# Moving modulation blocks, regrouping the solved values of a recurrent scan, and re-pacing projections in a two-layer hybrid block

## The chip, the cores and the metric

The kernel runs on one core of a Trainium2 chip. The metric is the device time of one execution in microseconds (us), and the median of several runs is compared. Engines are named as in the profile: PE is TensorE's matmul side and PEld its weight loads, DVE is VectorE, ACT is ScalarE, POOL is GpSimd, SP is SyncE, whose queue issues most transfers. PEclk is the granted share of TensorE's clock: 1.0 is 2.4 GHz and 0.5 is 1.2 GHz, the only two levels, so a value between them is a mean over a stretch.

## The reference

Two layers work on 512 tokens (256 of context, 256 latent) of width 1024. In each layer:

- `m = silu(cond) @ ada_w + ada_b` gives six modulation vectors per conditioning (shift, scale and gate of the mixer, shift, scale and gate of the MLP), 6 x 1024 columns, so 12 blocks of 512 columns.
- `h = rms_norm(x) * (1 + scale) + shift`, then `p = h @ w_in`, some 13,000 columns.
- Three mixers read `p`: an SSD (Mamba) mixer, an RWKV-7 scan in both directions over 16 heads of 64, and a gated delta net (GDN) in both directions over 8 heads of 128.
- `mixed = g_m*(y_m@w_bm) + g_r*(y_r@w_br) + g_g*(y_g@w_bg)` with sigmoid gates out of `p`; `x += gate1 * (mixed @ w_out)`; then `x += gate2 * (relu(h2@w_ff1)^2 @ w_ff2)` with `h2` modulated again.

Layer 1 needs only the 256 latent tokens from the mixers' outputs on, so there most products behind the scans are half as long. All is float32; large products are made of three passes with operands split in a high and a low part.

## The kernel before

**Order.** Every part is a Python generator that yields after a piece of work. `weave` (line 30) merges generators: it always steps the one with the smallest `(steps done + 0.5) / weight`, and the tile framework schedules the merged program on the engines. Each engine then runs its instructions in a fixed order.

**Stages of a layer**, as `run` (line 1580) writes them:

1. The pre-stage (drain at line 1644): `scalars` (decays), `first` (the low-rank parts of RWKV, its gates and the first 36 steps of the RWKV chain `rc`) and `ada(li, range(4, 12), ...)`, the modulation blocks 4 to 11 of this layer. Blocks 0 to 3 (shift and scale of the mixer) are made earlier: layer 0's before the layers, layer 1's in the MLP of layer 0.
2. The mix (line 1648): `rc` with weight 400 (about 460 steps are left in layer 0), `gc`, the GDN chain, with weight 195 (some 224 steps), and `ahead`, 44 projections with weight 48.
3. `merge` of the RWKV and the GDN branch, woven with `mamba_chain`; then `merge` of the Mamba branch; then `w_out`.
4. `mlp`: four groups of eight `w_ff1` and eight `w_ff2` products.

**`ada`** (line 235). One block loads four 512 KB pieces of `ada_w` (`araw`), multiplies them as 32 float32 products with 32 weight columns, copies the sums (`adaS`), transposes them and adds the bias into `modT`. In the pre-stage its loads are issued by POOL, with two buffers; elsewhere by SP with four.

**`proj` and `ahead`**. `proj` loads 1024 x 128 of `w_in` in two pieces (`wraw`), splits each (ACT writes `whi`, POOL writes `wlo`) and makes 24 products over 512 or 256 tokens. `ahead` (line 1249) makes 24 gate projections ("t", with a tanh), 8 of Mamba's z ("z") and 12 with a convolution ("c"), and stores them in device memory for the stage behind the mix. They come in eight groups of three t, one z, and one or two c.

**`rwkv_scan`** (line 837). One of 16 units (head pair x half) is eight steps, each with two directions `d` and two heads `e`: four products `rA<-U,W` give the solved values; each of the four results stands in its own 32 partitions of `rA`, and four ACT copies (lines 852 and 853) bring them into `U`; four products `rA<-U,KT` give the next state; DVE multiplies by the decay into the next step's `U`. The profile counts each of these float32 products as two instructions.

Of the kernel before, what the change touches and what calls it, by code (L numbers as in the profile page):

```python
# [8 lines left out]
F32 = mybir.dt.float32  # L9
F32R = mybir.dt.float32r  # L10
AF = mybir.ActivationFunctionType
ALU = mybir.AluOpType
# [17 lines left out]
def weave(*parts):  # L30

    live = [[g, n, 0] for g, n in parts]
    while live:
        p = min(live, key=lambda e: (e[2] + 0.5) / e[1])
        p[2] += 1
        try:
            next(p[0])
        except StopIteration:
            live.remove(p)
            continue  # L40
        yield


def drain(g):
    for _ in g:
        pass

L0, N0, N1, W_S, W_R, W_F, W_G = 3, 16, 20, 24, 400, 48, 195
W_A = 4


class Hybrid:
# [182 lines left out]
    def ada(self, li, blocks, pool, bufs=4, tag=None):  # L235

        condT = self.condT
        if condT is None:
            condT = pool.tile([128, 8, 32], F32, name="condR")
            self.dma(condT, self.condD)  # L240
        for b in blocks:
            new = (lambda nm: self.gen([128, 128], nm)) if tag is None else (lambda nm: self.sp.tile([128, 4, 128], F32, tag=tag, name=nm)[:, 0])
            ps = new("adaps")
            for kk in range(4):
                raw = pool.tile([128, 2, 512], F32, tag="araw", name="araw", bufs=bufs)
                (self.nc.gpsimd if tag else self.nc.sync).dma_start(out=raw, in_=self.ins["ada_w"][li][256 * kk : 256 * kk + 256, 512 * b : 512 * b + 512].rearrange("(k p) n -> p k n", p=128))
                for k in range(2):
                    for j in range(4):
                        self.mm(ps[32 * j : 32 * j + 32, :], condT[:, 2 * kk + k, :], raw[:, k, 128 * j : 128 * j + 128],
                                start=(kk + k == 0), stop=(kk == 3 and k == 1))  # L250
            S = pool.tile([128, 128], F32, tag="adaS", name="adaS", bufs=bufs // 2)
            self.nc.scalar.copy(S, ps)
            pt = new("adaT")
            self.tr(pt, S)
            v = pt.rearrange("p (j r) -> p j r", r=32)[:, :, 0:2]
            o = 48 * li + 4 * b
            self.tt(self.modT[:, li, 4 * b : 4 * b + 4, :], v, self.bcol[:, o : o + 4].unsqueeze(2).to_broadcast([128, 4, 2]), ALU.add)
            yield
# [578 lines left out]
    def rwkv_scan(self, li, hp, q, S, Unext):  # L837

        nc, rp = self.nc, self.rp
        skip = q == 0 and li == NL - 1  # L840
        U, W, KT, PC = S["U"], S["W"], S["KT"], S["PC"]
        sl = slice(256 * q, 256 * q + 256)
        A = self.rA
        y = None
        for s in range(8):
            cc = (s, 7 - s)
            for d in range(2):
                for e in range(2):
                    o = slice(64 * d + 32 * e, 64 * d + 32 * e + 32)
                    self.mm(A[o, 0:64], W[:, e, 0, d, cc[d]], U[:, e, cc[d]])  # L850
            for d in range(2):
                nc.scalar.copy(U[96:128, 0, cc[d]], A[64 * d : 64 * d + 32, 0:64])  # L852
                nc.scalar.copy(U[32:64, 1, cc[d]], A[64 * d + 32 : 64 * d + 64, 0:64])  # L853

            Un, cn = (U, (s + 1, 6 - s)) if s < 7 else (Unext, (0, 7))
            f = 0 if cn[0] < cn[1] else 1
            if not (q == 1 and s == 7):
                for d in range(2):
                    y0 = 64 if d == f else 128
                    for e in range(2):  # L860
                        self.mm(A[64 * e : 64 * e + 64, y0 : y0 + 64], KT[:, e, 8 * d + cc[d]], U[:, e, cc[d]])


            if not skip and s % 4 == 3:
                for e in range(2):
                    for d in range(2):
                        g = (s // 4) ^ d
                        y0 = 192 + 128 * g + 64 * e
                        for i in range(4):
                            self.mm(A[32 * i : 32 * i + 32, y0 : y0 + 64], W[:, e, 1, d, 4 * g + i], U[:, e, 4 * g + i])  # L870
                if y is None:
                    y = rp.tile([128, 4, 64], F32, tag="ry", name="ry")
                    yf = y.rearrange("p a b -> p (a b)")
                    nc.scalar.copy(yf, A[:, 192:448])
                else:
                    self.tt(yf, yf, A[:, 192:448], ALU.add)

            if not (q == 1 and s == 7):
                lo, hi = min(cn), max(cn)
                i, j = 8 * f + cc[f], 8 * (f + 1) + cc[1 - f]  # L880
                for e in range(2):
                    o = slice(64 * e, 64 * e + 64)
                    dec = fap(PC[o], [[j - i, 2], [0, 64]], i)
                    self.vlast = self.tt(Un[o, e, lo : hi + 1 : hi - lo], A[o, 64:192].rearrange("p (d v) -> p d v", d=2), dec).ins
            yield
        if skip:
            return
        gT = rp.tile([128, 256], F32, tag="gT", name="gT")
        self.load(gT, self.gD[li][128 * hp : 128 * hp + 128, sl])
        st = rp.tile([128, 3, 4], F32, tag="rst", name="rst")  # L890
        nc.vector.tensor_reduce(out=st[:, 0], in_=y, axis=AX.X, op=ALU.add)
        self.ts(st[:, 0], st[:, 0], 1.0 / 64)
        self.tt(y, y, st[:, 0].unsqueeze(2).to_broadcast([128, 4, 64]), ALU.subtract)
        ys = rp.tile([128, 4, 64], F32, tag="ryT", name="rys")
        self.act(ys, y, AF.Square)
        nc.vector.tensor_reduce(out=st[:, 1], in_=ys, axis=AX.X, op=ALU.add)
        self.ts(st[:, 1], st[:, 1], 1.0 / 64, ALU.mult, 64e-5, ALU.add)
        self.rsqrt(st[:, 2], st[:, 1], 4)
        self.tt(y, y, st[:, 2].unsqueeze(2).to_broadcast([128, 4, 64]))
        yield  # L900
        py = self.gen([128, 256], "ryT")
        for j in range(2):
            self.tr(py[:, 128 * j : 128 * j + 128], yf[:, 128 * j : 128 * j + 128])
        yT = rp.tile([128, 256], F32, tag="ryT", name="ryT")
        self.act(yT, py, AF.Identity, bias=self.pc["r_ln_b"][:, hp : hp + 1], scale=self.pc["r_ln_g"][:, hp : hp + 1])
        self.tt(yT, yT, S["bT"], ALU.add, eng=nc.gpsimd)
        self.tt(yT, yT, gT, eng=nc.gpsimd)
        self.dma(self.yD[li][1][128 * hp : 128 * hp + 128, sl], yT)
        yield
# [334 lines left out]
        self.dma(self.yD[li][2][128 * h : 128 * h + 128, t0:], yT[:, t0:])  # L1244
        yield

    N_AH = 44

    def ahead(self, li):


        nc, gp = self.nc, self.gp
        t0 = 256 if li == NL - 1 else 0
        todo = []
        for i in range(8):
            todo += [("t", 3 * i + j) for j in range(3)] + [("z", i)] + [("c", 3 * i // 2 + j) for j in range(1 + i % 2)]
        for kind, n in todo:
            new = lambda: gp.tile([128, T], F32, tag="gzs", name="ahead")
            rows = slice(128 * n, 128 * n + 128)
            if kind == "z":  # L1260
                o = new()
# [318 lines left out]
    def run(self):  # L1580
# [4 lines left out]
        with ExitStack() as ctx:  # L1585
# [38 lines left out]
            for li in range(dbg.get("layers", NL)):  # L1624
                end = ExitStack()
                with lay[li] as s:
                    with ExitStack() as s2:
# [8 lines left out]
                        with self.pool(f"pre{li}") as pre:  # L1636
# [4 lines left out]
                                yield from weave((lo, 10 - L0), (itake(rc, N0), N0))  # L1641
                                yield from weave((self.rwkv_gates(li, pre), 8), (itake(rc, N1), N1))

                            drain(weave((self.scalars(li, pre), W_S), (first(), 18 + N0 + N1), (self.ada(li, range(4, 12), pre, 2, "gsc"), W_A)))
                        self.ig = s2.enter_context(self.pool(f"ig{li}"))
                        self.gp = s2.enter_context(self.pool(f"gp{li}"))
                        gc = self.gdn_chain(li) if "g" in which else iter(())
                        drain(weave((rc, W_R), (self.ahead(li), W_F), (gc, W_G)))
                    mixed_p = s.enter_context(self.pool(f"mx{li}"))
                    mixed = mixed_p.tile([128, 8, T], F32, name="mixed")  # L1650
                    flip = [0]
# [27 lines left out]
                    mf = end.enter_context(self.psum(f"mf{li}", 4, side="right"))  # L1679
                    x = xp.tile([128, 8, T], F32, name="x")  # L1680
                    self.dma(x, xD)
                    drain(self.merge(li, 0, "w_bm", bp, mixed, False, eng))
                    self.raw_bufs, self.wp, self.mp = 3, wf, mf
                    with self.pool(f"wo{li}") as op:
                        drain(self.w_out(li, x, mixed, op, eng))
                    self.dump(f"x1_{li}", x)
                if li < NL - 1:
                    wp = open_layer(li + 1)
                with end:
                    with self.pool(f"fm{li}") as mp:  # L1690
                        with self.pool(f"ae{li}") as ap:
                            ad = self.ada(1, range(4), ap) if li == 0 else iter(())
                            if li < NL - 1:
                                self.params(li + 1, ap)
                            drain(weave((self.mlp(li, x, mp, eng), self.N_F), (ad, 4)))
                        self.dump(f"x2_{li}", x)
                        if li < NL - 1:
                            self.dma(xD, x)
# [5 lines left out]
def itake(g, n):  # L1704

    for _ in range(n):
        try:
            next(g)
        except StopIteration:
            return  # L1710
        yield
# [27 lines left out]
```

## Time and profile before

| | |
|---|---|
| Median of 3 runs | 4058.03 us (4052.08 to 4059.62) |
| Profiled execution | 4078.95 us, its span 4077.2 us, mean granted clock 0.865 |
| Busy share of the span | PE 85%, PEld 64%, DVE 59%, POOL 54%, ACT 43% |
| Transfers | 468.79 MB, mean 115 GB/s |

The span is what the profiler saw between the first and the last instruction; 1.75 us lie around it. A busy share counts an instruction from its start to its modelled end, and matmuls overlap, so PE's share says how seldom it stood still, not how near it was to its peak. The stages can be told apart by their instructions: in layer 0 the pre-stage runs to about 300 us, the mix to 1515, the merges and `w_out` to 1857, the MLP to 2270; in layer 1 the pre-stage ends at about 2490 and the mix at 3610.

### The profile page before, as it was taken

What the parts mean: (1) busy time and instruction counts of PE and PEld (TensorE: products, weight loads), DVE (VectorE), ACT (ScalarE), POOL (GpSimd) and SP (SyncE); (2) the same over time, 40 slices, a digit from 0 to 9 for tenths busy, and PEclk for the clock granted to TensorE, in tenths of its full rate; (3) what the DMA queues carried; (4) which work ended last, traced back from release to release, by engine and by line L of the source; (5) the groups of instructions that cost most, each with busy time, mean ns of one, the idle gap of its engine ahead of it and who ended that gap; (6) DMA issues with size and microseconds to landing.
All of it is one profiled execution on the core that took longest, in us unless ns stands there. A gap on an engine that the chain in (4) does not pass through costs nothing. (4 is left out here: it accounts for less than half of the span.)

```text
span 4077.2 us, 71668 instructions
## 1 busy us (share of the span) xinstructions
PE 3455.8 (85%) x25827; PEld 2598.3 (64%) x25827; DVE 2421.4 (59%) x5836; ACT 1758.9 (43%) x4025; POOL 2191.6 (54%) x2882
## 2 busy tenths in 40 slices
PE   5778989999989869988999677788878878768798
PEld 3556666666766645666887446666667666546697
DVE  2557766776667746644333635776666766746465
ACT  2345545555556422223222334545555545322343
POOL 3448765856758403433443445767656857324354
PEclk7879989989989758989999876878988888669799
DMA  6753434434433126444332573334334433154464
GB/s 199 208 155 88 105 92 103 102 97 104 108 98 96 48 53 175 129 142 145 96 103 73 153 227 94 95 89 112 94 95 104 100 94 85 39 140 129 131 170 131
DMA packets 789775, 468.79 MB, mean 115 GB/s; under 512 B 243116, under 2 KB 736172, under 8 KB 788908
## 3 DMA queue, kind: packets, MB, share of 16 engines
q1 hardware_dynamic: 780204, 430.66, 39.6%
q0 software_dynamic: 9216, 33.56, 2.7%
q8 instruction: 203, 3.33, 0.4%
q14 instruction: 152, 1.25, 0.1%
HBM read 384.64 MB, written 79.43 MB: 114 GB/s over the span
## 5 line engine op out<-in xcount | busy, mean ns | idle before, releaser
L75 POOL TENSOR_TENSOR wlo<-wraw,whi 128x512 fp32r<-128x512 f32 (+1 forms) x576 | 948.5, 1649 | 840.0 <-ACT whi L198 793.4
L198 ACT CAST whi<-wraw 128x512 fp32r<-128x512 f32 (+1 forms) x608 | 454.8, 751 | 920.6 <-PE pj L87 282.8
L87 PE MATMUL pj<-hhi,whi 128*128 128x512 f32 (+2 forms) x1664 | 676.1, 406 | 78.9 <-ACT ahead L72 21.6
L87 PE MATMUL pj<-hhi,wlo 128*128 128x512 f32 (+2 forms) x1664 | 659.0, 396 | 7.8 <-POOL wlo L75 7.8
L87 PE MATMUL pj<-hlo,whi 128*128 128x512 f32 (+2 forms) x1664 | 649.5, 390 | 2.8 <-DVE hlo L84 2.8
L87 PEld LDWEIGHTS pj<-hhi,whi 128*128 128x128 f32 (+1 forms) x1664 | 348.4, 209 | 160.4 <-ACT ahead L72 25.0
L87 PEld LDWEIGHTS pj<-hhi,wlo 128*128 128x128 f32 (+1 forms) x1664 | 346.7, 208 | 78.7 <-POOL wlo L75 10.6
L75 POOL TENSOR_TENSOR cpr<-cpr 128x512 f32<-128x512 f32 (+1 forms) x288 | 365.1, 1268 | 50.1 <-ACT cpr L72 39.6
L87 PEld LDWEIGHTS pj<-hlo,whi 128*128 128x128 f32 (+1 forms) x1664 | 349.1, 210 | 55.5 <-DVE hlo L84 4.5
L72 ACT ACTIVATE cpr<-cin,ptab 128x512 f32<-128x512 f32 (+1 forms) x360 | 240.1, 695 | 38.9 <-POOL cpr L75 30.4
L75 DVE TENSOR_TENSOR invP<-invP,invT 128x60 f32<-128x60 f32 (+24 forms) x992 | 213.9, 216 | 24.6
L75 DVE TENSOR_TENSOR invT<-invP,invL 128x60 f32<-128x60 f32 (+24 forms) x992 | 205.8, 207 | 26.1 <-DMA invL<-invM 1.5
L87 PE MATMUL rA<-U,W 128*32 128x64 f32 x3584 | 142.9, 255 | 89.7 <-DVE U L75 84.0
L75 DVE TENSOR_TENSOR U<-rA,PC 64x128 f32<-64x128 f32 x480 | 137.2, 286 | 129.8 <-PE rA L87 89.6
L75 DVE TENSOR_TENSOR fr<-fr 128x512 f32<-128x512 f32 (+1 forms) x64 | 135.4, 2124 | 85.1 <-ACT fr L72 85.1
L87 PEld LDWEIGHTS rA<-U,W 128*32 128x32 f32 x3584 | 79.1, 122 | 164.6 <-DVE U L75 104.3
L75 POOL TENSOR_TENSOR invT<-invY,invL 128x60 f32<-128x60 f32 (+24 forms) x496 | 164.8, 332 | 32.5 <-DMA invL<-invM 7.4
L75 POOL TENSOR_TENSOR invY<-invY,invT 128x60 f32<-128x60 f32 (+24 forms) x496 | 167.4, 338 | 25.8
L87 PE MATMUL f<-fhi,whi 128*128 128x512 f32 (+1 forms) x512 | 171.8, 340 | 6.2 <-ACT whi L198 4.2
L87 PE MATMUL rA<-U,KT 128*64 128x64 f32 x1920 | 130.0, 261 | 54.6 <-ACT U L853 53.3
L852 ACT COPY U<-rA 32x64 f32<-32x64 f32 x512 | 102.9, 201 | 169.7 <-PE rA L87 150.6
L87 PE MATMUL f<-hhi,whi 128*128 128x512 f32 (+1 forms) x512 | 173.5, 343 | 2.7 <-ACT whi L198 1.6
(398 smaller groups left out, 7973.9 us busy)
## 6 DMA issues: line engine op xcount, KB each, us to landing
wraw<-in_w_in SPq DMA_DIRECT2D x412, 256.0 KB
wraw<-in_w_ff SPq DMA_DIRECT2D x128, 512.0 KB
araw<-in_ada_w POOLq DMA_DIRECT2D x64, 512.0 KB, 5.6
invL<-invM SPq DMA_DIRECT2D x192, 128.0 KB
araw<-in_ada_w SPq DMA_DIRECT2D x32, 512.0 KB
lD<-lo SPq DMA_DIRECT2D x64, 256.0 KB
dupD<-ahead SPq DMA_DIRECT2D x40, 256.0 KB
rcs<-lD SPq DMA_DIRECT2D x32, 256.0 KB
```

The lines of the kernel that those rows point to most:

```text
L72: return self.nc.scalar.activation(out, in_, func, bias=bias, scale=scale, **kw)
L75: return (eng or self.nc.vector).tensor_tensor(out=out, in0=a, in1=b, op=op)
L87: return self.nc.tensor.matmul(out, lhsT, rhs, start=start, stop=stop, **kw)
L198: self.nc.scalar.copy(hi, raw)
L852: nc.scalar.copy(U[96:128, 0, cc[d]], A[64 * d : 64 * d + 32, 0:64])
```

## The change

There are three parts.

- **Modulation blocks.** `ada` leaves the pre-stage of both layers. Layer 0's blocks 4 to 7 are woven into the merge of the Mamba branch and 8 to 11 into `w_out`; layer 1's blocks 4 to 11 go into the MLP of layer 0, beside its blocks 0 to 3. All loads of these blocks are now issued by SP.
- **Solved values.** The results of both directions of one head stand side by side in the 32 partitions where `U` wants them, so two ACT copies of 32 x 128 take the place of four of 32 x 64. The columns of `rA` behind them move by 64.
- **Pace of `ahead`.** A group is now one or two c, one z and one or two t; the other gate projections come last. `weave` takes a function as a weight: the first 30 items are spread over keys 0 to 0.93 and the last 14, all gate projections or nearly so, over 0.93 to 1.14.

```diff
-        p = min(live, key=lambda e: (e[2] + 0.5) / e[1])
+        p = min(live, key=lambda e: e[1](e[2]) if callable(e[1]) else (e[2] + 0.5) / e[1])
...
+N_AH, P_AH, P_END = 30, 0.93, 1.14
...
-            for d in range(2):
-                for e in range(2):
-                    o = slice(64 * d + 32 * e, 64 * d + 32 * e + 32)
-                    self.mm(A[o, 0:64], W[:, e, 0, d, cc[d]], U[:, e, cc[d]])
-            for d in range(2):
-                nc.scalar.copy(U[96:128, 0, cc[d]], A[64 * d : 64 * d + 32, 0:64])
-                nc.scalar.copy(U[32:64, 1, cc[d]], A[64 * d + 32 : 64 * d + 64, 0:64])
+            g0 = 0 if cc[0] < cc[1] else 1
+            dc = slice(min(cc), max(cc) + 1, max(cc) - min(cc))
+            for e in range(2):
+                o = slice(96 - 64 * e, 128 - 64 * e)
+                for d in range(2):
+                    x0 = 0 if d == g0 else 64
+                    self.mm(A[o, x0 : x0 + 64], W[:, e, 0, d, cc[d]], U[:, e, cc[d]])
+            for e in range(2):
+                o = slice(96 - 64 * e, 128 - 64 * e)
+                nc.scalar.copy(U[o, e, dc], A[o, 0:128].rearrange("p (d v) -> p d v", d=2))
...
+    def ahead_at(k):
+        return (k + 0.5) / N_AH * P_AH if k < N_AH else P_AH + (k - N_AH + 0.5) / (44 - N_AH) * (P_END - P_AH)
...
-        todo = []
+        todo, gates = [], [*range(8, 24), *range(8)]
         for i in range(8):
-            todo += [("t", 3 * i + j) for j in range(3)] + [("z", i)] + [("c", 3 * i // 2 + j) for j in range(1 + i % 2)]
+            todo += [("c", 3 * i // 2 + j) for j in range(1 + i % 2)] + [("z", i)] + [("t", gates.pop(0)) for j in range(1 + i % 2)]
+        todo += [("t", n) for n in gates]
...
-                            drain(weave((self.scalars(li, pre), W_S), (first(), 18 + N0 + N1), (self.ada(li, range(4, 12), pre, 2, "gsc"), W_A)))
+                            drain(weave((self.scalars(li, pre), W_S), (first(), 18 + N0 + N1)))
...
-                        drain(weave((rc, W_R), (self.ahead(li), W_F), (gc, W_G)))
+                        drain(weave((rc, W_R), (self.ahead(li), self.ahead_at), (gc, W_G)))
...
+                        ad = self.ada(0, range(4, 12), ap) if li == 0 else iter(())
+                        drain(weave((self.merge(li, 0, "w_bm", bp, mixed, False, eng), self.N_G), (itake(ad, 4), 4)))
...
+                            drain(weave((self.w_out(li, x, mixed, op, eng), 9), (ad, 4)))
...
-                            ad = self.ada(1, range(4), ap) if li == 0 else iter(())
+                            ad = self.ada(1, range(12), ap) if li == 0 else iter(())
...
-                            drain(weave((self.mlp(li, x, mp, eng), self.N_F), (ad, 4)))
+                            drain(weave((self.mlp(li, x, mp, eng), self.N_F), (ad, 12)))
```

## Rows read from the trace of the kernel before

**Rows 1.** Busy us of each engine by stage (count), granted clock, DMA share, GB/s

```profile
core 0: us, PE busy (x) PEld busy (x) DVE busy (x) ACT busy (x) POOL busy (x), PEclk, DMA share, GB/s
75.00:300.00 225.00, 173.03 (x1205) 117.55 (x1205) 112.19 (x255) 93.94 (x194) 114.78 (x178) 0.82 0.62 179
300.00:1290.00 990.00, 897.18 (x7273) 663.72 (x7274) 679.93 (x1834) 528.78 (x1267) 692.00 (x1008) 0.93 0.39 98
1290.00:1515.00 225.00, 176.56 (x1666) 122.18 (x1664) 145.53 (x457) 89.54 (x269) 86.27 (x135) 0.70 0.20 50
1857.00:2270.00 413.00, 388.16 (x1848) 301.64 (x1848) 157.94 (x209) 124.67 (x178) 151.28 (x64) 0.97 0.34 103
2270.00:2490.00 220.00, 165.41 (x1197) 121.05 (x1197) 105.99 (x238) 89.95 (x188) 110.71 (x177) 0.76 0.66 185
2490.00:3430.00 940.00, 781.22 (x6752) 616.88 (x6752) 646.78 (x1858) 504.08 (x1288) 635.71 (x991) 0.84 0.39 97
3430.00:3610.00 180.00, 136.70 (x1291) 97.86 (x1291) 108.92 (x352) 71.17 (x223) 62.22 (x123) 0.68 0.16 38
```

**Rows 2.** Stores of `ahead`, each mix: ns min/median/max, first and last start

```profile
L94 SPq DMA_DIRECT2D xcD<-ahead x10: 348/706/717, 412.9 to 1290.2; - x10
...
L94 SPq DMA_DIRECT2D xcD<-ahead x10: 338/718/1245, 2599.9 to 3430.6; - x10
```

**Rows 3.** The stages again, only instructions of the modulation blocks' sums (`adaps`)

```profile
75.00:300.00 225.00, 24.84 (x512) 14.56 (x512) 2.12 (x8) 0.82 0.62 179
...
2270.00:2490.00 220.00, 27.55 (x512) 16.04 (x512) 2.13 (x8) 0.76 0.66 185
...
1857.00:2270.00 413.00, 11.71 (x256) 7.58 (x256) 1.04 (x4) 0.97 0.34 103
```

**Rows 4.** PE's waits in 75:300, 2270:2490, 1857:2270, 1666:1770: us, times, longest

```profile
PE adaps L87 <- DMA araw<-in_ada_w: 12.1, 10, 2.8
...
PE adaps L87 <- DMA araw<-in_ada_w: 12.3, 9, 4.4
...
PE adaps L87 <- DMA araw<-in_ada_w: 3.3, 2, 2.1
...
PE yp L87 <- ACT yhi L1460: 11.7, 3, 8.9
```

**Rows 5.** Both mixes up to `ahead`'s end, only the projections' instructions (`pj`)

```profile
300.00:1290.00 990.00, 558.12 (x2066) 397.65 (x2067) 8.87 (x13) 64.63 (x123) 0.93 0.39 98
...
2490.00:3430.00 940.00, 436.43 (x2088) 351.69 (x2088) 5.42 (x13) 51.18 (x117) 0.84 0.39 97
```

**Rows 6.** Timeline of DVE in layer 0's MLP: residuals, one per 24 products

```profile
2031.86 0.88 DVE L84 SCALAR_TENSOR_TENSOR x<-f,modT,x 128x256 f32<-128x256 f32 x2 [1.46 <-PE f L87]
...
2065.45 0.88 DVE L84 SCALAR_TENSOR_TENSOR x<-f,modT,x 128x256 f32<-128x256 f32 x2 [4.73 <-PE f L87]
```

**Rows 7.** Groups of one product in 300:1290 and 1290:1515: busy, mean ns | idle

```profile
L87 PE MATMUL gF<-gVP,gKE 64*128 64x128 f32 x168 | 41.9, 330 | 5.4 <-DVE gS L84 3.8 <-ACT gVP L72 1.4
...
L87 PE MATMUL gF<-gVP,gKE 64*128 64x128 f32 x56 | 18.9, 432 | 5.1 <-DVE gS L84 2.6 <-ACT gVP L72 2.5
```

**Rows 8.** PE's waits in 2490:3430, the longest in total

```profile
PE rA L87 <- DVE U L75: 49.0, 38, 5.9
```

**Rows 9.** Timeline of PE: `rA` products at granted clock 1.0, then 0.5

```profile
923.31 0.32 PE L87 MATMUL rA<-U,W 128*32 128x64 f32 x8
...
924.59 0.45 PE L87 MATMUL rA<-U,KT 128*64 128x64 f32 x8
...
1388.95 0.44 PE L87 MATMUL rA<-U,W 128*32 128x64 f32 x8
...
1390.67 0.69 PE L87 MATMUL rA<-U,KT 128*64 128x64 f32 x8
```

**Rows 10.** ACT copies over the whole span, shapes apart: count | busy, mean ns

```profile
L852 ACT COPY U<-rA 32x64 f32<-32x64 f32 x512 | 102.9, 201 | 169.7 <-PE rA L87 150.6 <-DVE invP L75 5.5 <-DVE gS L84 2.9
...
L1120 ACT COPY gXT<-gq 32x128 f32<-32x128 f32 x32 | 8.1, 255 | 16.9 <-PE gq L87 16.5
```

More of the change, by code (lines that the diff above doesn't have):

```diff
@@ L250, in ada @@
                                 start=(kk + k == 0), stop=(kk == 3 and k == 1))
-            S = pool.tile([128, 128], F32, tag="adaS", name="adaS", bufs=bufs // 2)
+            S = pool.tile([128, 128], F32, tag="adaS", name="adaS", bufs=(bufs + 1) // 2)
             self.nc.scalar.copy(S, ps)
@@ L858, in rwkv_scan @@
                 for d in range(2):
-                    y0 = 64 if d == f else 128
+                    y0 = 128 if d == f else 192
                     for e in range(2):
@@ L867, in rwkv_scan @@
                         g = (s // 4) ^ d
-                        y0 = 192 + 128 * g + 64 * e
+                        y0 = 256 + 128 * g + 64 * e
                         for i in range(4):
@@ L873, in rwkv_scan @@
                     yf = y.rearrange("p a b -> p (a b)")
-                    nc.scalar.copy(yf, A[:, 192:448])
+                    nc.scalar.copy(yf, A[:, 256:512])
                 else:
-                    self.tt(yf, yf, A[:, 192:448], ALU.add)
+                    self.tt(yf, yf, A[:, 256:512], ALU.add)
             if not (q == 1 and s == 7):
@@ L883, in rwkv_scan @@
                     dec = fap(PC[o], [[j - i, 2], [0, 64]], i)
-                    self.vlast = self.tt(Un[o, e, lo : hi + 1 : hi - lo], A[o, 64:192].rearrange("p (d v) -> p d v", d=2), dec).ins
+                    self.vlast = self.tt(Un[o, e, lo : hi + 1 : hi - lo], A[o, 128:256].rearrange("p (d v) -> p d v", d=2), dec).ins
             yield
@@ L1245, in gdn_finish @@
         yield
-    N_AH = 44
+    @staticmethod
+    def ahead_at(k):
+        return (k + 0.5) / N_AH * P_AH if k < N_AH else P_AH + (k - N_AH + 0.5) / (44 - N_AH) * (P_END - P_AH)
     def ahead(self, li):
@@ L1681, in run @@
                     self.dma(x, xD)
[L1682 to L1685, printed above, removed]
+                    with self.pool(f"ao{li}") as ap:
+                        ad = self.ada(0, range(4, 12), ap) if li == 0 else iter(())
+                        drain(weave((self.merge(li, 0, "w_bm", bp, mixed, False, eng), self.N_G), (itake(ad, 4), 4)))
+                        self.raw_bufs, self.wp, self.mp = 3, wf, mf
+                        with self.pool(f"wo{li}") as op:
+                            drain(weave((self.w_out(li, x, mixed, op, eng), 9), (ad, 4)))
                     self.dump(f"x1_{li}", x)
```

## The prediction

> **What bounds the kernel now.** I read the busy table by stage first [rows 1]. In both layers most of the time is the mix: 990 + 225 us in layer 0, 940 + 180 us in layer 1. Each mix has two parts, and the stores of `ahead` show the border: the last one is issued at 1290.2 and at 3430.6 us [rows 2], 81% of the way through, because its last item has the key 43.5/48 = 0.91 while both chains run to a key of about 1.15. Up to there PE is busy for 897 of 990 us at a granted clock of 0.93 in layer 0, and for 781 of 940 at 0.84 in layer 1. Behind it PE is busy 78% and 76% at 0.70 and 0.68, POOL only 38% and 35%: what is left are the two scans, whose small steps wait on each other. In the pre-stages DMA is at 0.62 and 0.66, far above the mix's 0.39, and PE stands for 52 and 55 us. The MLP of layer 0 is nearly full (388 of 413 us at 0.97), so whatever PE gets there costs its time.
>
> So the body of layer 0's mix is near PE's limit, its tail is bound by the chains, layer 1's mix lies between, and the pre-stages are a mixture of transfers and short waits.
>
> All terms below are made against the profiled execution (4078.95 us, of which 4077.2 are the span) and taken off the median, 4058.03, unscaled; the two are 0.5% apart. Less than 0.2% (8 us) from the median counts as no change, about what a measurement of this kernel can tell.
>
> **Modulation blocks, what is freed.** Each pre-stage loses eight blocks: 512 PE instructions, 24.8 and 27.6 us of busy time [rows 3], and PE's waits for their data, 12.1 and 12.3 us [rows 4]. Together 37 + 40 = 77 us. PE works in order, so this delayed everything behind it, but another wait (for the stores of the low-rank parts, or for a decay) will end later in part of these places, since PE stands for some 40 us more in each pre-stage than those data waits explain. Bounds: 40% (31 us), if chains off PE take over, and 100 us, if the lighter DMA load (16 of some 40 MB less in each) shortens other waits too. I take 80%, nearest to PE's own rows: 62 us.
>
> **Modulation blocks, what they cost later.** The four blocks that are already in the MLP take 11.7 us of PE [rows 3] and 3.3 us of waits for data [rows 4]: 2.9 to 3.8 us a block. Sixteen blocks arrive: four with the last merge, four with `w_out`, eight in the MLP. 16 x 2.9 = 47 us. The merge stands for 11.7 us waiting for `yhi` [rows 4], room for its four blocks (11.7 us), so 47 - 12 = 35. Bounds: 24, if MLP joints hide some of the rest, and 60 (16 x 3.8), if nothing is hidden. Their 64 loads move from POOL's queue to SP's, where a load that waits for its buffer (four, so one block) holds the weight loads behind it, and with them `whi` on ACT and then PE; the 3.3 us above are such a place, and the 60 holds it. Net of both: -62 + 35 = **-27 us**.
>
> **Pace of `ahead`, the body.** No projection is added or dropped; 14 of 44 move behind the others. Body of layer 0: 558.1 us for 2066 products [rows 5], so 86 projections at 6.5 us; in the MLP, where nothing else intervenes, six groups of 24 take 33.6 us [rows 6], 5.6 us each. Fourteen are 91 us of busy PE. Layer 1's 436.4 us hold about 35 full ones; 436.4 - 35 x 6.5 over 52 gives 4.0 us for a half-length one, and its 14 are 56 us. A projection also carries its weight split (ACT, POOL), but these have slack beside PE. How much of 91 and 56 comes back is the main unknown: nothing, if the chains set the pace, or all, if PE does. PE's idle share, 9% in layer 0 and 17% in layer 1, lies near the PE end in the first and between the ends in the second. I take 65% of 91 (59 us) and 45% of 56 (25 us).
>
> **Pace of `ahead`, the tail.** The same work lands in 225 and 180 us. It needs 91 and 56 us and finds PE standing for 48 and 43 us [rows 1]; I let 60% of that be filled (29 and 26 us), since a gap of a scan step is shorter than a projection's 24 products. The tail also runs at a low clock after PE's gaps: one and the same product takes 432 ns there and 330 ns in the body [rows 7]. With PE fed between the steps, I expect the clock nearer the body's, which shortens the chains' own PE time (137 us without projections in layer 0) by some 15%: 20 us, and 15 us in layer 1. Growth: 91 - 29 - 20 = 42, and 56 - 26 - 15 = 15 us. Bounds: 0, and all 147. Net: -(59 + 25) + (42 + 15) = **-27 us**. The chains stay the last to end, so the merges begin as before. Convolutions at the head of each group put ACT and POOL work earlier, at the same density; I cost this at nothing, under PE's 91% in the body; without that cover it is a few us at the mix's start.
>
> **Solved values.** There are 256 steps (two instructions of line 852 each, 512 in all [rows 10]). Four copies in a row take 4 x 0.20 and the gaps, 0.86 us; one of 32 x 128 out of PSUM takes 0.255 [rows 10], so two take 0.52: 0.34 us less for ACT and for the chain behind it. In exchange both directions of a head now share 32 columns of PE. In the old form all four products ran side by side, eight instructions in 0.32 us at full clock and 0.44 at half; the state products, which use two column strips with two products each, as the new ones will, take 0.45 and 0.69 [rows 9]. So +0.13 or +0.25 us: a step's chain gets shorter by 0.21 us at full clock and 0.09 at half. PE's waits for `U` (49 us in layer 1's body alone [rows 8]) say that the chain often matters; I count half the steps at 0.16: 20 us. But PE is held longer by 256 x 0.13 = 33 us, of which I count 40%, where PE is the limit: 13 us. Net **-7 us**, bounds -54 (all steps gain, at full clock) and +33.
>
> The Trainium skill speaks against this part (TensorEngine Tiling (Array Packing), Key Properties): different tiles of the array load and multiply in parallel, so products that share a tile gain nothing from that. By it the solve takes four turns where it took two, as the state products' rows show.
>
> **Sum.** -27 - 27 - 7 = -61 us: 4058 - 61 = **3997 us**. Own range of this case: 3960 to 4038.
>
> **Rivals.**
>
> *PE is the body's only limit.* Then all 147 us come back while the tail still grows by 57: -90, with the other parts -124: 3934 us. PE's 91% at 0.93 in layer 0 speaks for it, 49 us of waits for `U` in layer 1 [rows 8] against it.
>
> *The projections are not kept back.* They depend on nothing in the chains, so the framework's scheduler may put them into earlier gaps; the tail stays empty and the body full. Then only the other two parts count: -34, 4024 us. Against it: in the trace of before they ended at 81%, just where their keys put them.
>
> *The pre-stage's waits only change names.* Freed 31, costs 35, and the pace gives nothing: +4 - 7, about 4055 us. For it: PE's many other short waits there; against it: DMA falls by nearly half.
>
> *The tail pays in full (slower).* PE takes instructions in order, and a block of 24 products (5.6 us [rows 6]) before a scan step delays it and ACT's copy, DVE's decay and the next step after it. If the tails grow by all 147 us and the bodies give back 40% (59), the pace costs +88, with the other parts +54: 4112 us. It decides for slower as soon as the tails grow by 42 us more than the bodies shrink (34 us of other gains and 8 us of tolerance). For it: the tail's steps are chains; against it: POOL idle for more than half, and the low clock.
>
> **Chances.** Forecast 0.55; PE the only limit 0.14; not kept back 0.09; waits change names 0.11; tail pays in full 0.11. Of the fourth I put 0.08 within 0.2% and 0.03 below it; the others lie clearly on their sides. Faster: 0.55 + 0.14 + 0.09 + 0.03 = 0.81; same 0.08; slower 0.11. The range leaves out the slower case and a part of the second (its times below 3925, with the solve's gain at its bound): 3925 to 4058.
>
> **What would show it.** Right: pre-stages 25 to 40 us shorter each, with no `adaps` before 1600 us; in the MLP of layer 0 about 23 us more; the last gate stored within 20 us of the mix's end; the granted clock of the tails above 0.8; tails longer by 15 to 45 us and bodies shorter by more; copies of 32 x 128 at about 255 ns, 512 of them; the solve's eight instructions at about 0.45 us. Wrong: a body as long as before with fewer projections in it (the chains set the pace), a tail that grows by 90 us or more, weight loads of the MLP or the last merge late behind waiting `araw` loads, or a solve that takes more than 0.5 us at full clock.

## The result and the profile after

| | median us (lowest to highest) | ratio to the kernel before, 95% interval |
|---|---|---|
| before, in the same comparison | 4058.82 (4052.08 to 4068.97), 4 runs | |
| after | 3994.22 (3989.24 to 3996.23), 4 runs | 0.9840 (0.9825 to 0.9854) |

The change takes 64.6 us off the median. The forecast was 61 us, 3997 us. That agreement is partly luck: two of its three terms were off, by 14 and by 18 us, in opposite directions.

To see where the time went I cut both traces at the same seven instructions. These are the marks of the kernel after; the columns are duration in ns (min/median/max), then first and last start in us. A stage ends with the last start of its row, the mix with the first start of `mXX` (the merge's first load).

```profile
L95 SPq DMA_DIRECT2D gD<-go x8: 319/341/394, 236.7 to 262.4; - x8
L99 SPq DMA_DIRECT2D mXX<-dupD x16: 319/422/582, 1472.1 to 1596.8; - x16
L76 DVE TENSOR_TENSOR mixed<-mixed,tg x16: 691/692/2842, 1636.0 to 1790.3; 128x512 f32<-128x512 f32 x16
L85 DVE SCALAR_TENSOR_TENSOR x<-op,modT,x x16: 473/480/486, 1796.9 to 1838.1; 128x256 f32<-128x256 f32 x16
L85 DVE SCALAR_TENSOR_TENSOR x<-f,modT,x x64: 473/480/485, 1920.6 to 2248.6; 128x256 f32<-128x256 f32 x64
L95 SPq DMA_DIRECT2D gD<-go x8: 344/388/433, 2428.4 to 2451.7; - x8
L99 SPq DMA_DIRECT2D mXX<-dupD x16: 382/430/2407, 3545.6 to 3619.0; - x16
```

The same marks in the kernel before, where the mixes begin and end:

```profile
L94 SPq DMA_DIRECT2D gD<-go x8: 320/345/423, 259.0 to 285.3; - x8
L98 SPq DMA_DIRECT2D mXX<-dupD x16: 319/430/907, 1514.8 to 1635.8; - x16
L94 SPq DMA_DIRECT2D gD<-go x8: 344/386/436, 2454.8 to 2478.0; - x8
L98 SPq DMA_DIRECT2D mXX<-dupD x16: 339/427/1582, 3610.6 to 3689.3; - x16
```

The stage lengths that follow, in us, for these two and for three of the experiments below:

| Stage | before | after | change | e1 | e6 | e11 |
|---|---|---|---|---|---|---|
| start and pre-stage, layer 0 | 285.3 | 262.4 | -22.9 | 261.6 | 259.8 | 264.7 |
| mix, layer 0 | 1229.5 | 1209.7 | -19.8 | 1241.2 | 1202.7 | 1210.5 |
| merges, layer 0 | 303.1 | 318.2 | +15.1 | 311.4 | 301.5 | 315.0 |
| `w_out`, layer 0 | 38.5 | 47.8 | +9.3 | 48.9 | 38.4 | 47.8 |
| MLP, layer 0 | 393.0 | 410.5 | +17.5 | 409.5 | 392.1 | 393.4 |
| pre-stage, layer 1 | 228.6 | 203.1 | -25.5 | 201.8 | 205.0 | 204.3 |
| mix, layer 1 | 1132.6 | 1093.9 | -38.7 | 1095.7 | 1089.6 | 1058.0 |
| rest, layer 1 | 466.6 | 448.6 | -18.0 | 466.9 | 447.4 | 465.3 |

The profiled execution of before lies 20 us above the median of its runs, so this table's changes sum to 83 us where the medians differ by 65. It tells in which stages time moved; what a part is worth is taken from medians.

In the profile the blocks' move frees 20 us (layer 0's pre-stage alone, without its start) and 26 us, and costs 15 + 9 + 18 = 42 us later. The mixes and what follows them in layer 1 give the rest. Not all of this is the pace: e1, which has the pace of before, has layer 1's mix at 1095.7 us too.

Busy time by stage of the kernel after (columns as in [rows 1]): the pre-stage, the mix up to the end of the first 30 projections, the rest of the mix; for layer 0, then its MLP, then layer 1.

```profile
72.00:278.00 206.00, 147.88 (x677) 102.36 (x677) 113.75 (x249) 92.53 (x180) 93.36 (x149) 0.82 0.41 120
278.00:1235.00 957.00, 861.23 (x7099) 637.93 (x7100) 702.16 (x1888) 486.08 (x1067) 678.93 (x1004) 0.91 0.37 93
1235.00:1472.00 237.00, 211.58 (x1852) 153.85 (x1848) 124.44 (x402) 92.38 (x218) 102.77 (x138) 0.93 0.31 80
1838.00:2270.00 432.00, 404.54 (x2369) 314.43 (x2369) 160.48 (x222) 127.47 (x188) 151.17 (x65) 0.97 0.45 137
2270.00:2464.00 194.00, 143.17 (x677) 105.98 (x677) 104.70 (x231) 87.22 (x175) 88.83 (x147) 0.74 0.46 122
2464.00:3310.00 846.00, 715.80 (x6315) 559.70 (x6315) 621.19 (x1790) 448.41 (x1035) 587.97 (x945) 0.85 0.39 95
3310.00:3545.00 235.00, 180.89 (x1743) 141.04 (x1743) 130.97 (x423) 92.89 (x232) 114.99 (x172) 0.80 0.35 86
```

Beside [rows 1] the reader is to see three things. The DMA share of the pre-stages fell from 0.62 and 0.66 to 0.41 and 0.46, but PE stands there as long as before: 206 - 148 = 58 us against 52 in layer 0, 51 against 55 in layer 1. The tail of layer 0's mix is now as full as its body: PE is busy 89% (78% before) at a granted clock of 0.93 (0.70 before). Layer 1's tail is at 0.80 (0.68 before), and 77% busy (76% before).

What the projections (`pj`) have of it, in the two bodies and the two tails of the kernel after, answers to [rows 5]:

```profile
278.00:1235.00 957.00, 495.71 (x1776) 349.19 (x1776) 9.54 (x14) 56.94 (x110) 0.91 0.37 93
1235.00:1472.00 237.00, 114.58 (x432) 81.23 (x432) 1.36 (x2) 11.23 (x19) 0.93 0.31 80
2464.00:3310.00 846.00, 378.29 (x1766) 294.56 (x1766) 5.76 (x14) 46.59 (x104) 0.85 0.39 95
3310.00:3545.00 235.00, 73.80 (x443) 61.63 (x442) 0.82 (x2) 7.65 (x19) 0.80 0.35 86
```

So the projections were kept back: 290 products fewer in layer 0's body, and 432, eighteen projections, in its tail.

Single operations of the kernel after: the stores of the gates, both mixes (as [rows 2]); `gF` in layer 0's tail, then layer 1's (count, busy us, mean ns, as [rows 7]); the solve's eight instructions at granted clock 1.0 and at 0.5 (as [rows 9]); the copy into `U` (as [rows 10]).

```profile
L95 SPq DMA_DIRECT2D tD<-ahead x48: 319/344/1142, 338.7 to 3506.9; - x48
...
L88 PE MATMUL gF<-gVP,gKE 64*128 64x128 f32 x56 | 14.2, 335 | 0.1
...
L88 PE MATMUL gF<-gVP,gKE 64*128 64x128 f32 x60 | 16.4, 357 | 1.0 <-ACT gVP L73 1.0
...
922.28 0.42 PE L88 MATMUL rA<-U,W 128*32 128x64 f32 x8 [1.47 <-DVE U L76]
...
927.43 0.65 PE L88 MATMUL rA<-U,W 128*32 128x64 f32 x8
...
L858 ACT COPY U<-rA 32x128 f32<-32x128 f32 x512 | 132.0, 258 | 163.5 <-PE rA L88 126.1 <-DVE invP L76 9.6 <-DVE gR L85 5.3
```

The last gate is stored 39 us before layer 1's mix ends (3545.6 - 3506.9), and 46 us before layer 0's. `gF` went from 432 to 335 ns in layer 0's tail, because the clock is higher there. The solve takes 0.42 us where it took 0.32, at half clock 0.65 where it took 0.44.

PE's waits in the kernel after: the three longest of the pre-stage of layer 0, then for the blocks' data in the last merge, in `w_out` and in the MLP (total us, times, longest us, as [rows 4]):

```profile
PE rhob L92 <- DVE rex L664: 10.3, 2, 8.7
PE pj L88 <- ACT rkv L73: 6.0, 4, 2.3
PE lora L88 <- ACT ghi L199: 5.4, 1, 5.4
...
PE adaps L88 <- DMA araw<-in_ada_w: 10.6, 4, 9.8
...
PE adaps L88 <- DMA araw<-in_ada_w: 3.7, 3, 3.2
...
PE adaps L88 <- DMA araw<-in_ada_w: 4.2, 3, 1.8
```

The wait for `araw` left the pre-stage, and other waits stand in its place. In the last merge PE waited for `yhi` before [rows 4]; now one wait of 9.8 us for the first block's weights stands there.

### The profile page after: what moved, and what is told of

It reads as the page before. It is cut to its first block, busy times and chain, and to the rows that moved or that the text cites. A ratio compares the mean times of both kernels' runs of the same rounds, so it can differ in the third digit from the quotient of the medians.

```text
span 3994.2 us, 71116 instructions
## 1 busy us (share of the span) xinstructions
PE 3410.8 (85%) x25827; PEld 2578.4 (65%) x25827; DVE 2409.5 (60%) x5836; ACT 1680.1 (42%) x3513; POOL 2155.6 (54%) x2818
## 5 line engine op out<-in xcount | busy, mean ns | idle before, releaser
L88 PE MATMUL rA<-U,W 128*32 128x64 f32 x3584 | 171.3, 241 | 91.5 <-DVE U L76 89.2
L88 PEld LDWEIGHTS rA<-U,W 128*32 128x32 f32 x3584 | 108.2, 118 | 164.4 <-DVE U L76 105.0
L858 ACT COPY U<-rA 32x128 f32<-32x128 f32 x512 | 132.0, 258 | 163.5 <-PE rA L88 126.1
L88 PE MATMUL f<-fhi,wlo 128*128 128x512 f32 (+1 forms) x512 | 170.8, 338 | 5.0 <-DVE wlo L76 3.7
```

The source lines that it names most:

```text
L88: return self.nc.tensor.matmul(out, lhsT, rhs, start=start, stop=stop, **kw)
L858: nc.scalar.copy(U[o, e, dc], A[o, 0:128].rearrange("p (d v) -> p d v", d=2))
```

## The experiments

Three parts of the change are called the blocks, the pace (with the new order of the items) and the solve. The theory to test was the forecast's own sum: blocks -27, pace -27, solve -7. Its rivals were that the pace gives nearly all (the pre-stage's waits only change names), and that something outside the three parts matters. The kernel before ran beside each: median 4056.42 us (23 runs) beside e1 to e4, 4056.12 (11) beside e5 to e8, 4053.99 (11) beside e9 to e12.

### One part at a time

**e1: the blocks alone.** The four edits of the diff that concern `ada`; `ahead`, `weave` and `rwkv_scan` as before.

> The kernel before with the moved modulation blocks alone. Theory 1 (the prediction's terms): 62 us freed in the pre-stages, 35 us paid later, so 27 us less, about 4031 us. Theory 2 (from the landmarks of the two traces: pre-stages 20 and 25 us shorter; last merge, w_out and MLP of layer 0 together 43 us longer): freed and paid nearly cancel, within 10 us of the kernel before.

Measured: 4041.94 us, ratio 0.9969 (0.9957 to 0.9982), -13 us by the ratio: half of the forecast's 27, and nearer to theory 2's 10.

**e2: the pace and the new order alone.**

```diff
+N_AH, P_AH, P_END = 30, 0.93, 1.14
...
-                        drain(weave((rc, W_R), (self.ahead(li), W_F), (gc, W_G)))
+                        drain(weave((rc, W_R), (self.ahead(li), self.ahead_at), (gc, W_G)))
```

> The kernel before with the new pace and order of the projections alone. Theory 1: 27 us less, about 4031 us, two thirds of it in layer 0. Theory 2: the pace carries nearly all of the mixes' gain of 60 us, 40 to 55 us less, about 4010 us, two thirds of it in layer 1. If only the solve made layer 1's mix shorter, this run stays above 4040 us.

Measured: 4012.72 us, ratio 0.9890 (0.9870 to 0.9909), -45 us. More than the forecast's 27, less than the rival's 90.

**e3: the solve alone.** Only the edits in `rwkv_scan`.

> The kernel before with the two wide copies in place of four alone. Theory 1: 7 us less, about 4051 us, within the 8 us that count as no change. Theory 2 (the solve carries layer 1's mix): 25 us or more less, 4033 us or below. A loss of up to 33 us, if only the longer stay on PE counts.

Measured: 4050.39 us, ratio 0.9985 (0.9969 to 1.0002), -6 us. The interval reaches beyond 1, so a gain is not shown.

**e4: pace and solve, without the blocks.**

> The changed kernel with the modulation blocks left in the pre-stages (pace and solve alone). Theory 1: 34 us less than before, about 4024 us. Theory 2: the blocks' move is worth nothing, so this run is within 10 us of the changed kernel, about 3995 to 4005 us.

Measured: 3994.18 us, ratio 0.9850 (0.9826 to 0.9873), -61 us. Alone the parts give 13 + 45 + 6 = 64 us, and all of them together 65. But e4 has all but 4 us of the gain already, so on top of the other two the blocks add little, and the solve adds 16 to the pace's 45. The intervals reach from 5 to 10 us to either side, and those of e2 and e4 overlap: too wide to settle how 20 us are shared between these two.

### What the blocks cost and free

**e5: the kernel before, without blocks 4 to 11 in either layer.**

```diff
+        nc.vector.memset(self.modT, 0.0)
...
-                            drain(weave((self.scalars(li, pre), W_S), (first(), 18 + N0 + N1), (self.ada(li, range(4, 12), pre, 2, "gsc"), W_A)))
+                            drain(weave((self.scalars(li, pre), W_S), (first(), 18 + N0 + N1)))
```

> The kernel before without modulation blocks 4 to 11 of both layers (modT is set to zero; the gates and the second modulation are left out of the result). It measures what the blocks cost in the pre-stages. Theory 1 (the prediction): 62 us less than before, about 3994 us. Theory 2 (from the landmarks of four traces: pre-stages 20 to 22 and 26 to 27 us shorter): 47 us less, about 4009 us.

Measured: 4001.13 us, ratio 0.9867 (0.9848 to 0.9885), -54 us: what the sixteen blocks cost where they stood. The forecast had 62.

**e6: the kernel after, without the same blocks.**

```diff
-                        ad = self.ada(0, range(4, 12), ap) if li == 0 else iter(())
+                        ad = iter(())
...
-                            ad = self.ada(1, range(12), ap) if li == 0 else iter(())
+                            ad = self.ada(1, range(4), ap) if li == 0 else iter(())
...
-                            drain(weave((self.mlp(li, x, mp, eng), self.N_F), (ad, 12)))
+                            drain(weave((self.mlp(li, x, mp, eng), self.N_F), (ad, 4)))
```

> The changed kernel without the sixteen moved blocks (modT is set to zero where they would write; gates and second modulation are left out of the result). It measures what the blocks cost at their new places. Theory 1: 35 us less than the changed kernel, about 3959 us. Theory 2 (last merge 8 to 10, w_out 10, MLP 18 us longer in the traces): 37 to 43 us less, about 3954 us.

Measured: 3952.35 us, ratio 0.9741 (0.9721 to 0.9762), 42 us less than the kernel after by the medians and 40 by the ratios. The forecast had 35. In the table of stages e6 has the merges (301.5), `w_out` (38.4) and the MLP (392.1) near their lengths of before. The three together are 44.5 us shorter than in the kernel after (732.0 against 776.5), so the 42 us lie there. -54 + 42 = -12; e1 measured -13.

### Which half of the pace does it

**e7: the new order of the items, at the old even weight of 48.**

```diff
-        todo = []
+        todo, gates = [], [*range(8, 24), *range(8)]
...
-            todo += [("t", 3 * i + j) for j in range(3)] + [("z", i)] + [("c", 3 * i // 2 + j) for j in range(1 + i % 2)]
+            todo += [("c", 3 * i // 2 + j) for j in range(1 + i % 2)] + [("z", i)] + [("t", gates.pop(0)) for j in range(1 + i % 2)]
+        todo += [("t", n) for n in gates]
```

> The kernel before with the new order of the projections (convolutions first, most gates last) at the old even pace. If filling the tails is what helps, this gains nothing: within 8 us of before, 4056 us. If the order itself helps (the convolutions' ACT and POOL work earlier, the merges of layer 1 served sooner), it keeps part of the 45 us of pace and order together: 4035 us or less.

Measured: 4076.40 us, ratio 1.0051 (1.0033 to 1.0068), 20 us slower than before, which neither of the two expectations has.

**e8: the new pace, with the old order of the items.**

> The kernel before with the new pace at the old order, so that the last 14 items hold gates, z and convolutions alike. If filling the tails with PE work is what helps, most of the 45 us stay: 4010 to 4025 us. If it must be the gates, because convolutions load ACT, POOL and DVE beside the scans, less than half stays: 4035 us or more.

Measured: 4011.50 us, ratio 0.9895 (0.9874 to 0.9917), -43 us, within 2 us of e2. So the keys alone carry the gain. What kind of projection is kept back makes no difference that these runs can tell, and the 20 us that the order costs at even spacing are not there at the new pace. Why it costs them was not tested.

### Body and tail apart

**e9: the kernel before with 14 gate projections fewer in each layer.** Each of the fourteen is a memset on POOL and its store.

```diff
+            elif kind == "t" and n in (18, 19, 20, 21, 22, 23, 0, 1, 2, 3, 4, 5, 6, 7):
+                o = new()
+                nc.gpsimd.memset(o[:, t0:], 0.0)
+                self.dma(self.tD[li][rows, t0:], o[:, t0:])
```

> The kernel before without fourteen of its gate projections (the same that the changed kernel keeps for the end; zeros are stored in their place, so these gates are left out of the result). It measures what fourteen projections cost in the bodies of the mixes. Theory 1 (the prediction): 59 + 25 = 84 us less than before, about 3972 us. Theory 2 (PE is the bodies' only limit): 147 us less, about 3909 us. Theory 3 (the chains set the pace): under 40 us less.

Measured: 3974.62 us, ratio 0.9795 (0.9771 to 0.9819), -83 us; the forecast's two body terms sum to 84.

**e10: e2 with the last 14 of each mix left out in the same way.**

> The kernel with the new pace and order alone (4013 us) without its last fourteen projections (zeros are stored in their place). It measures what they cost in the tails. Theory 1: 42 + 15 = 57 us less, about 3956 us. Theory 2: the tails swallow them nearly whole, 30 us or less, 3983 us or more, and this explains that pace and order together gave 44 us where 27 were expected. If the tails cost 57 us, the bodies must have given about 100.

Measured: 3934.32 us, ratio 0.9709 (0.9683 to 0.9734), -118 us against before, and 78 less than e2 (73 by the ratios). So with the other 30 spread as the change spreads them, the bodies give back 118 us and the tails take 73 to 78: the net 45 of e2 out of two larger numbers than the forecast's 84 and 57. e9 does the same work as e10 and is 40 us slower; its 30 items stand in the old order and unevenly, with holes where the 14 were. So of the 118 us, 83 come with leaving the fourteen out, and 35 (by the ratios; 40 by the medians) with order and spacing of the other thirty. The two were not taken apart; e7 has the new order evenly spaced over all items, and lost 20 us by it. Neither of the two theories for e10 reached as low as 3934 us.

The marks of the mixes in e2, then in e9, then in e10 (columns as above) tell the layers apart:

```profile
L95 SPq DMA_DIRECT2D gD<-go x8: 320/345/422, 259.1 to 285.2; - x8
L99 SPq DMA_DIRECT2D mXX<-dupD x16: 320/424/792, 1506.6 to 1630.3; - x16
L95 SPq DMA_DIRECT2D gD<-go x8: 344/384/443, 2447.9 to 2471.0; - x8
L99 SPq DMA_DIRECT2D mXX<-dupD x16: 320/430/2195, 3559.0 to 3635.0; - x16
```

```profile
L94 SPq DMA_DIRECT2D gD<-go x8: 320/345/422, 255.5 to 282.0; - x8
L98 SPq DMA_DIRECT2D mXX<-dupD x16: 319/425/1504, 1466.8 to 1585.6; - x16
L94 SPq DMA_DIRECT2D gD<-go x8: 344/386/430, 2408.0 to 2431.2; - x8
L98 SPq DMA_DIRECT2D mXX<-dupD x16: 319/430/1227, 3505.1 to 3586.5; - x16
```

```profile
L95 SPq DMA_DIRECT2D gD<-go x8: 319/344/422, 254.5 to 279.1; - x8
L99 SPq DMA_DIRECT2D mXX<-dupD x16: 320/424/433, 1457.1 to 1582.1; - x16
L95 SPq DMA_DIRECT2D gD<-go x8: 338/384/1516, 2391.9 to 2415.0; - x8
L99 SPq DMA_DIRECT2D mXX<-dupD x16: 319/428/2547, 3466.4 to 3545.3; - x16
```

Layer 0's mix is 1506.6 - 285.2 = 1221.4 us in e2, 1184.8 in e9 and 1178.0 in e10, so the tail's 14 cost 43 (e2 against e10). Before, e1, e3 and e5, with the old pace and order, have 1228 to 1241, mean 1234, so the body gave 1234 - 1178 = 56 in e10, and 49 in e9.

In layer 1 I take the mix together with the rest, since the rest alone is 447 to 454 us long in some kernels and 461 to 469 in others, at either pace: 1539.3 us in e2 (1088.0 + 451.3), 1542.9 in e9, 1517.6 in e10, and 1563 to 1566 in e1, e3 and e5. The kernel before is left out of this mean: its one profile has 1599.2, in an execution 20 us above the kernel's median. So the body gave some 47 in e10, but only 21 in e9, where the same fourteen are missing, and the tail cost 22, or 37 by the mix alone. Since layer 1's mix is 37 us longer in before than in e1, at the same pace, its numbers are worth less than layer 0's.

That the pace shortens both layers doesn't hang on one pair of profiles. Layer 0's mix is 1228 to 1251 us in the five kernels with the old pace and all projections (before, e1, e3, e5, e7) and 1203 to 1226 in the seven with the new pace and all projections (after, e2, e4, e6, e8, e11, e12); mix and rest of layer 1 are 1563 to 1599 in the former and 1523 to 1551 in the latter.

### Two versions that follow

**e11: layer 1's blocks 4 to 11 in layer 1's own last merge and `w_out`**, as layer 0's are, and MLP 0 with four blocks as before.

```diff
-                        ad = self.ada(0, range(4, 12), ap) if li == 0 else iter(())
+                        ad = self.ada(li, range(4, 12), ap)
...
-                            ad = self.ada(1, range(12), ap) if li == 0 else iter(())
+                            ad = self.ada(1, range(4), ap) if li == 0 else iter(())
...
-                            drain(weave((self.mlp(li, x, mp, eng), self.N_F), (ad, 12)))
+                            drain(weave((self.mlp(li, x, mp, eng), self.N_F), (ad, 4)))
```

> The changed kernel with layer 1's blocks 4 to 11 in the last merge and w_out of layer 1, like layer 0's, and not in the MLP of layer 0. If a block costs its PE time wherever it stands, the 18 us saved in the MLP come back in layer 1: 3994 us. If layer 1's last merge has room (PE stands for 27 us of its last 82 before the MLP, for yhi and the norm), 8 to 15 us less: 3980 to 3986 us.

Measured: 3960.84 us (3956.04 to 3963.72), ratio 0.9768 (0.9745 to 0.9792): the fastest kernel here that does all of the work, 33 us below the kernel after by the medians and 29 by the ratios. That is below both expectations, and the blocks explain little of it. In the table the MLP gets 17 us back and layer 1's rest is 17 us longer; the blocks are 23 us of busy PE there, but e8, e10 and e12 have as long a rest without them. The gain stands in layer 1's mix, 1094 to 1058 us, whose code is the same. These rows are its window and PE's longest wait in it, first in the kernel after, then in e11:

```profile
2452.00:3546.00 1094.00, 905.42 (x8112) 707.65 (x8112) 761.32 (x2228) 549.49 (x1285) 710.44 (x1132) 0.84 0.39 94
...
PE rA L88 <- DVE U L76: 67.0, 48, 6.2
```

```profile
2436.00:3494.00 1058.00, 900.34 (x8093) 701.35 (x8093) 752.23 (x2225) 544.24 (x1277) 707.33 (x1127) 0.85 0.39 96
...
PE rA L88 <- DVE U L76: 37.1, 38, 3.4
```

PE's work is the same, 905 and 900 us; what differs is that it stands 189 us in the one and 158 in the other, and 30 of these 31 us are its waits for `U`. Up to layer 0's MLP, where the edit begins, both traces have PE's 11954 instructions in the same order, but for four places; in layer 1's mix most stand in another place. That this order is why `U` comes earlier was not tested by itself.

**e12: 20 projections kept back in place of 14** (`N_AH = 24`).

> The changed kernel with 20 items kept for the end instead of 14. If the bodies are still closer to PE's limit than the tails, another 10 to 20 us less: 3974 to 3984 us. If the tails are full at fourteen (PE stands for 25 of 237 us in layer 0's), no change or slower: 3990 us or more.

Measured: 4012.76 us, ratio 0.9899 (0.9878 to 0.9921), 19 us more than the kernel after. Layer 0's mix is 16 us longer (1226.1 against 1209.7). Its stretch after the first 24 projections:

```profile
1180.00:1488.00 308.00, 279.95 (x2276) 204.49 (x2275) 168.42 (x478) 129.72 (x294) 151.17 (x183) 0.92 0.33 88
```

PE is busy for 280 of 308 us, 91%, at 0.92. With fourteen the tail was already at 89%, so there was little left to fill. That the full tail is what costs the time, and not the wider spacing of the first 24 items, is the likelier reading and was not tested.

## Why the prediction came out right, and where it was wrong

**The sum.** Forecast -27 -27 -7 = -61; measured by the parts alone -13 -45 -6 = -64, and 65 for the whole. The sign of each part was right. The blocks were overrated by 14 us, the pace underrated by 18; that the sum came within 4 us is luck to that extent.

**"What is freed": 62, measured 54 (e5).** The mis-sized part is the 80% of PE's waits and busy time. What came free is about PE's busy time, 24.8 + 27.6 = 52.4 us, and not its standing: 52 to 58 us in layer 0, 55 to 51 in layer 1, though the waits of 12.1 and 12.3 us for `araw` [rows 4] are gone. Others are in their place, the longest for `rex`, 10.3 us. So the rival "waits only change names" was right about the waits, and wrong about the busy time and the pace. The pre-stages became 20 and 26 us shorter in the two profiles; 25 to 40 was expected. DMA's lighter load, about a third less of its share, bought nothing to be seen. No moved block's sums ran before 1714 us, as expected.

**"What they cost later": 35, measured 40 to 42 (e6).** The error is in the credit of 12 us for the last merge. I let four blocks fill the wait for `yhi` there; the wait is for the first block's weights instead, 9.8 us in one piece, and the merges grew by 15 us. The eight blocks of the MLP cost 17.5 us, 2.2 each, less than the 2.9 taken: twelve are 26.84 us busy where four were 11.71 [rows 3]. About 23 us were expected of them.

**The pace: -27, measured -45 (e2) and -43 (e8).** The two body terms, 59 + 25 = 84, are the price of leaving the fourteen out, and e9 measured 83 for that; by its profile 49 in layer 0 and 21 in layer 1. The step that failed stands beside them: the earlier convolutions were costed at nothing, and the spacing of the thirty items that stay has no term at all. With the same work as e9 in the new order and spacing, e10 is another 35 to 40 us shorter, 22 of them in layer 1's mix (1051.4 against 1073.9) and 7 in layer 0's (1178.0 against 1184.8), so that its bodies gave 56 and some 47. How much of this is spacing, how much order, and how much the way in which the scheduler then sorts the program is open.

The tails' term, 42 + 15 = 57, was too small as well: 73 to 78 by the medians, by the profiles 43 in layer 0, as forecast, and 22 to 37 in layer 1. So the bodies gave 118 where 84 was forecast, the tails took some 16 to 21 more, and the difference is the gain that exceeded the forecast. The waits for `U`, 49 us in layer 1's body [rows 8], were taken as a sign against PE as its limit; 53 us of them stand in the shorter body of the kernel after.

The pieces as the forecast cut them: the tails' stretches became 12 and 55 us longer (15 to 45 was expected), the bodies 33 and 94 shorter. The border of 81% is layer 0's; in layer 1 `ahead` ended at 84% (940 of 1120 us).

**The clock in the tail** rose, 0.70 to 0.93 and 0.68 to 0.80. Above 0.8 was expected for both; layer 1's is just at it.

**The solve: -7, measured -6 (e3)**, which is not clear of nothing. The sizes were right: 0.42 us at full and 0.65 at half clock (0.45 and 0.69 forecast from the state products [rows 9]), copies of 258 ns (255 [rows 10]), 512 of them. What no run tells is how the 20 us counted for the shorter chain and the 13 for the longer hold on PE came out. By the Trainium skill (TensorEngine Tiling (Array Packing), Key Properties) different tiles can load weights and multiply in parallel, so products on the same tile have nothing of that; the trace agrees in direction, 0.32 us to 0.42 for the same four products, though that is far from twice the time. On top of the pace the solve may be worth more, 16 us between e2 and e4.

**The rivals.** "PE is the body's only limit" comes out neither in its bodies (147; 83 in e9, 118 in e10) nor in its sum (-90, measured -45). "Not kept back" fell with the 432 `pj` products in layer 0's tail. "The tail pays in full" is half true: the tails took 73 to 78 of their 147 us, and the bodies gave more. The last gate was not stored within 20 us of the end, but 46 and 39 us before it. The keys ran to 1.14 and the chains to 1.15, so what follows the last gate should be the chains' own last steps.

**What stays open:** why e7's order costs 20 us at even spacing; why the thirty others run 35 to 40 us faster in e10 than in e9; how 20 us of gain are shared between blocks and solve when all three parts are together; why `U` comes 30 us earlier in e11.

## What to carry to other kernels

Where independent work is woven beside dependent chains, place it by where the engine still stands, and stop when that stretch is as full as the rest: 14 projections moved into a tail at 78%, with the other thirty spread anew, gave 45 us, and 20 of them lost 19 again. Give the order and spacing of what stays behind a term of its own: here the two together were worth 35 to 40 us. When a step is moved out of a stage, count on its busy time and not on the waits beside it, and look at what its own first load will wait for in the new place. Two large terms of opposite sign should each be measured by leaving the work out (e6, e9, e10), since their difference alone hides errors in both.

## What was not expected of the hardware and the schedule

- The same work on the same engine takes 40 us more or less by its order and spacing (e9 against e10: 30 projections for each mix, with holes and evenly).
- A stage whose code is untouched moves by some 36 us between two kernels. Layer 1's mix does so twice: after and e11 (1094 and 1058 us, at equal PE work and a clock of 0.84 and 0.85, nearly all of it PE's waits for one tile), and before and e1 (1132.6 and 1095.7). A stage difference of that size between two kernels' profiles isn't proof of the edit's own effect, and the median of one kernel isn't either, as e11's shows. Several kernels with the edit against several without it, as for the pace above, come nearer.
- Filling PE's gaps by more work made the work beside it faster: `gF` 432 to 335 ns in layer 0's tail, at a granted clock of 0.70 before and 0.93 after.
